# Staging tiles of two triangular inverses, the order of four tiles, and eighteen first convolution taps, in a one-core decoder layer

## The chip, the cores and the metric

The kernel runs on one core of a Trainium2 chip. The core has a matrix engine (TensorE, "PE" in the profile; its weight loads are shown apart as "PEld"), a vector engine (VectorE, "DVE"), an activation engine (ScalarE, "ACT"), GpSimd ("POOL") and SyncE ("SP"), which here issues the DMA transfers. Each engine runs its own instructions in the order in which the built program lists them, and waits on semaphores for the others. The metric is the time of one execution in microseconds; lower is better.

## The reference, cut to what matters

One decoder layer for a sequence of 1024 positions with 1024 channels. A combined projection of the modulated input feeds two mixers: a recurrent branch (convolution of width 4, RG-LRU, times a GeLU gate) and a Gated DeltaNet of 16 value heads on 8 key heads in chunks. Then follow merge gates, an output projection and a gated MLP. The parts that the change touches are these:

```python
def causal_dwconv(x, w):
    """Depthwise causal conv. x: (B, S, C), w: (K, C); y[t] = sum_k w[k] * x[t-K+1+k]."""
...
def chunk_gated_delta_rule(q, k, v, g, beta):
    ...
    kb = k * beta[..., None]
    A = jnp.where(strict, jnp.einsum('bhnid,bhnjd->bhnij', kb, k) * decay, 0.0)
    T = A + jnp.eye(c, dtype=F32)
    u = lax.linalg.triangular_solve(T, v * beta[..., None], left_side=True, lower=True)
    w = lax.linalg.triangular_solve(T, kb * jnp.exp(G)[..., None], left_side=True, lower=True)
...
def token_mixer(h, w_in, rg_conv_w, rg_conv_b, ...):
    proj = h @ w_in
    xr, gr, q, k, v, z, a_in, b_in, g_a, g_b = split_cols(proj, IN_SPLITS)
    xr = causal_dwconv(xr, rg_conv_w) + rg_conv_b
```

The triangular solves are done in the kernel by computing the inverses of unit triangular blocks of 64 x 64.

## The kernel before, in words

Every large product is made of matmuls of 128x512 outputs, three for each pair of tiles: each operand is split into a rounded part and a remainder, and lines 267, 268 and 269 multiply high by high, low by high and high by low. A weight tile is loaded by `load_w` (L254: a DMA into `wr`, a rounded copy `wh` on ACT, the remainder `wl` on DVE, both in the split helper, L200 and L201). One projection of a 128-channel tile takes 48 such matmuls, and its two halves go to two PSUM tiles of the tag `mm`, of which the first phase has four (L404). A PSUM tile is taken again only when its last reader is done.

The program has two phases up to the output projection. The first works through a list `ORDER` (L638 to L656): K is a key head, G a merge gate, Z an output gate of a value head, X a recurrent tile. It begins G K G K Z K G K, then Z K G K Z K G K, then X Z G X Z and so on, with the RG-LRU pieces (`lru`) between the X. The second phase (from L658) makes queries q and values v by the same projections and runs the chunks of the delta rule.

A key head (`key_head`, L490) projects, convolves with four taps on DVE (`conv`, L304: the first tap at L307, or at L309 where there is a bias, the others at L312), multiplies the tile with itself in 16 pieces on PE (L503, PSUM tag `pre`), scales the products on DVE (L509) and writes 64x64 blocks to DRAM (L518). An output gate (`z_steps`, L624) takes each half of a projection from PSUM through a tanh on ACT (L628, tile `th`) and a multiplication on DVE (L629, tile `z`), and stores it.

After every fourth key head `invert(b)` (L523) is emitted. It loads the blocks of eight heads as one tile `tri` (L527), 128 blocks of 64x64 with a block on each partition, and inverts them by 62 steps of two DVE instructions each (L531 into `tmp`, L533 back into `tri`). Then it clears the other triangle (L538, L540), stores the inverse (`inv_d`, L541), and also stores the transposed inverse: eight pieces `tmpT` of 64x512, copied alternately by ACT (L550) and DVE (L548), each followed by its DMA (L551).

What sets the order: a framework's scheduler decides the order of each engine's list when the program is built, from the program's order, priorities and the buffers. `invert` is emitted under `tc.high_priority(offset=-30000)` (L655), which lets its instructions be placed behind others. Each tile belongs to a tag with a fixed number of buffers, a ring, and a tile waits for the last use of the tile that had its buffer before. The rings that matter: `tri` and `tmp` of `tri_pool`, and the ring of half tiles (`half(...)`, 128x512, tag "hf") with four buffers in the first phase. From that ring come `sq`, `hi`, `lo` (the norm of a key, L337 and L345), `sg` (L560), `th` and `z` (L627). Large tiles (`g(...)`) come from a common area; when `tri_pool` is closed (L659) its place is free for the second phase, whose tiles `kT` (key heads loaded again) and `x` (inverses) are made in `beside_load` and `inverse_load`.

Of the kernel before, what the change touches and what calls it, by code (L numbers as in the profile page):

```python
# [9 lines left out]
F32 = mybir.dt.float32  # L10
F32R = mybir.dt.float32r
AF = mybir.ActivationFunctionType
# [4 lines left out]
P = 128  # L17
D = 1024
S = 1024
# [6 lines left out]
QKH = 8  # L26
VH = 16
CH = 128
NCH = S // CH
BK = 64  # L30
# [3 lines left out]
TJ = 8  # L34
# [56 lines left out]
def hybrid_layer_kernel(ctx: ExitStack, tc: tile.TileContext, xT, c, w_adaT, cols_in, rows_in,  # L91
                        w_in, w_ab, w_rg, w_pa, w_pb, w_out, w_gu, w_dn, out):
    nc = tc.nc
    V, A, G, T, DMA = nc.vector, nc.scalar, nc.gpsimd, nc.tensor, nc.sync
    uid = [0]

    def nm(s):
        uid[0] += 1
        return f"{s}_{uid[0]}"
# [12 lines left out]
    def g(shape=(P, S), dt=F32, name="g"):  # L112
        tag, bufs = cur["rings"].get(name, ("g", cur["g"]))
        t = cur["pool"].tile([P, S + 4], dt, tag=tag, bufs=bufs, name=nm(name))
        n = math.prod(shape[1:])
        t = t[0 : shape[0], 0:n]
        return t if len(shape) == 2 else t.rearrange("p (a b) -> p a b", a=shape[1])

    def half(name, dt=F32):
        return cur["pool"].tile([P, HALF], dt, tag="hf", bufs=cur["hf"], name=nm(name))  # L120
# [4 lines left out]
    def ct(shape, dt=F32, name="c"):  # L125
        return const.tile(list(shape), dt, name=nm(name))
# [3 lines left out]
    def col(name, i):  # L130
        o = COL[name] + i
        return cols[:, o : o + 1]
# [4 lines left out]
    tri_pool = tri_stack.enter_context(tc.tile_pool(name="tri_pool", bufs=1))  # L137
# [20 lines left out]
    def cst(v, name):  # L158
        t = ct([P, 1], name=name)
        G.memset(t, v)  # L160
        return t
# [3 lines left out]
    eps_rms = cst(4.0 * RMS_EPS, "eps_rms")  # L165
    eps_ln = cst(LN_EPS / (ALPHA * ALPHA), "eps_ln")
    floor = cst(SQRT_FLOOR, "floor")


    ada = ct([P, 48], name="ada")  # L170
# [128 lines left out]
    def conv_in():  # L299
        t = g((P, S + 4), name="cv")  # L300
        V.memset(t[:, 0:4], 0.0)
        return t

    def conv(t, taps, wcol, out_t, bias=None):  # L304
        o = 4 - (taps - 1)
        if bias is None:
            V.tensor_scalar(out=out_t, in0=t[:, o : o + S], scalar1=wcol(0), scalar2=None, op0=ALU.mult)  # L307
        else:
            V.tensor_scalar(out=out_t, in0=t[:, o : o + S], scalar1=wcol(0), scalar2=bias,  # L309
                            op0=ALU.mult, op1=ALU.add)  # L310
        for i in range(1, taps):
            V.scalar_tensor_tensor(out=out_t, in0=t[:, o + i : o + i + S], scalar=wcol(i), in1=out_t,  # L312
                                   op0=ALU.mult, op1=ALU.add)

    def silu2(x, th):

        A.activation(th, x, AF.Tanh, scale=0.5)
        V.scalar_tensor_tensor(out=x, in0=th, scalar=1.0, in1=x, op0=ALU.add, op1=ALU.mult)

    def qkv_tile(j):  # L320

        res = []
        for _ in qkv_steps(j, res):
            pass
        return res[0]

    def qkv_steps(j, res):
        cv = conv_in()
        yield from project_steps(
            w_in[T_Q + j], lambda ps, hf: A.activation(cv[:, 4 + hf * HALF : 4 + (hf + 1) * HALF], ps, AF.Copy))  # L330
        t = g(name="qkv")
        conv(cv, 4, lambda i: col("qkv_w", j * 4 + i), t)
        silu2(t, cv[:, 0:S])
        res.append(t)

# [44 lines left out]
    first_cv = {}  # L380
    with tc.tile_pool(name="ps_first", bufs=1, space=PSUM, reuse_waits="tile") as psf:
# [11 lines left out]
        for i in range(NFIRST):  # L393
            t = conv_in()
# [95 lines left out]
    def key_head(i):  # L490
        j = QKH + i
        if i in first_cv:
            t = g(name="k")
            conv(first_cv[i], 4, lambda q: col("qkv_w", j * 4 + q), t)
            silu2(t, first_cv[i][:, 0:S])
        else:
            t = qkv_tile(j)
        scale_by_norm(t, eps_l2, 1.0)
        DMA.dma_start(out=kT_d[i], in_=t)
        kk = [pre_ps() for _ in range(2)]  # L500
        for cc in range(NCH):
            s = t[:, cc * CH : (cc + 1) * CH]
            T.matmul(kk[cc // 4][:, (cc % 4) * CH : (cc % 4 + 1) * CH], s, s, start=True, stop=True)  # L503
        decs = [decay_rows(2 * i + hh) for hh in range(2)]
        ns = [d.rearrange("p (c i) -> p c i", c=NCH) for d in decs]
        for q in range(2):
            for hh in range(2):
                for cc in range(4 * q, 4 * q + 4):
                    V.scalar_tensor_tensor(  # L509
                        out=ns[hh][:, cc, :], in0=kk[q][:, (cc % 4) * CH : (cc % 4 + 1) * CH],  # L510
                        scalar=nbeta[:, cc, 2 * i + hh : 2 * i + hh + 1], in1=ns[hh][:, cc, :],
                        op0=ALU.mult, op1=ALU.mult)
        for hh in range(2):
            h = 2 * i + hh
            b, r = h // 8, h % 8
            n = ns[hh]
            for bl in range(2):
                DMA.dma_start(  # L518
                    out=blk_d[b][bl * BK + r * NCH : bl * BK + (r + 1) * NCH].rearrange("c j i -> j c i"),
                    in_=n[bl * BK : (bl + 1) * BK, :, bl * BK : (bl + 1) * BK])  # L520
            DMA.dma_start(out=off_d[h], in_=n[0:BK, :, BK : 2 * BK])

    def invert(b):  # L523

        flat_m = tri_pool.tile([P, BK * (BK + 1)], F32, tag="tri", name=nm("tri"))
        m = flat_m[:, 0 : BK * BK].rearrange("p (k i) -> p k i", k=BK)
        DMA.dma_start(out=m, in_=blk_d[b])  # L527
        for j in range(1, BK - 1):
            w = BK - 1 - j
            tmp = tri_pool.tile([P, 1024], F32, tag="tmp", name=nm("tmp"))[:, 0 : j * w].rearrange("p (k i) -> p k i", k=j)  # L530
            V.tensor_tensor(out=tmp, in0=m[:, 0:j, j : j + 1].to_broadcast([P, j, w]),  # L531
                            in1=m[:, j : j + 1, j + 1 :].to_broadcast([P, j, w]), op=ALU.mult)
            V.tensor_tensor(out=m[:, 0:j, j + 1 :], in0=m[:, 0:j, j + 1 :], in1=tmp, op=ALU.add)  # L533

        n = BK // 2
        while n:
            low = flat_m.rearrange("p (b x) -> p b x", x=2 * n * (BK + 1))[:, :, BK * n : 2 * BK * n]
            V.memset(low.rearrange("p b (r c) -> p b r c", c=BK)[:, :, :, 0:n], 0.0)  # L538
            n //= 2
        V.memset(flat_m[:, 0 : BK * BK : BK + 1], 1.0)  # L540
        DMA.dma_start(out=inv_d[b], in_=m)  # L541
        ts = tri_pool.tile([P, 1024], F32, tag="tmp", name=nm("tmpT"))[0:BK]
        for q in range(BK // TJ):
            o = q * TJ * BK % 1024
            t = ts[:, o : o + TJ * BK].rearrange("p (j k) -> p j k", j=TJ)
            src = m[0:BK, :, TJ * q : TJ * (q + 1)].rearrange("p k j -> p j k")
            if q % 2:
                V.tensor_copy(out=t, in_=src)  # L548
            else:
                A.activation(t, src, AF.Copy)  # L550
            DMA.dma_start(out=invT_d[b][:, TJ * q : TJ * (q + 1), :], in_=t)  # L551
# [18 lines left out]
    def xr_tile(t):  # L570
        cv = conv_in()
        project(w_in[T_XR + t], lambda ps, hf: A.activation(cv[:, 4 + hf * HALF : 4 + (hf + 1) * HALF], ps, AF.Copy))
        x = g(name="xr")
        conv(cv, 4, lambda i: col("rg_w", t * 4 + i), x, bias=col("rg_b", t))
        xr32[t] = x
        xrh[t], xrl[t] = split_hi_lo(x, "xr")

# [97 lines left out]
            T.matmul(psd[0:BK, cc * BK : (cc + 1) * BK], s[:, cc, :], x[BK:P, cc, BK : 2 * BK], start=True, stop=True)  # L675
        A.activation(x[0:BK, :, BK : 2 * BK], psd[0:BK, :].rearrange("p (c i) -> p c i", c=NCH), AF.Copy)

    def inverse_load(h):

        b, r = h // 8, h % 8  # L680
        x = g((P, NCH, CH), name="x")
        V.memset(x[BK:P, :, 0:BK], 0.0)
        parts = sm([BK, 2, HALF], tag="inv", bufs=2, name="inv")
        n_off, yT = (parts[:, q, :].rearrange("p (c i) -> p c i", c=NCH) for q in range(2))
        DMA.dma_start(out=n_off, in_=off_d[h])
        DMA.dma_start(out=yT, in_=invT_d[b][r * NCH : (r + 1) * NCH].rearrange("c j k -> j c k"))
        for bl in range(2):
            DMA.dma_start(out=x[bl * BK : (bl + 1) * BK, :, bl * BK : (bl + 1) * BK],
                          in_=inv_d[b][bl * BK + r * NCH : bl * BK + (r + 1) * NCH].rearrange("c j i -> j c i"))
        return x, n_off, yT  # L690
# [15 lines left out]
    def projections(i, st):  # L706

        yield from qkv_steps(i, st["q"])
        for h in (2 * i, 2 * i + 1):
            yield from qkv_steps(2 * QKH + h, st["v"])  # L710

    def beside_load(i, st):
        st["k"] = g(name="kT")
        DMA.dma_start(out=st["k"], in_=kT_d[i])
        st["inv"] = [inverse_load(h) for h in (2 * i, 2 * i + 1)]
        st["x"] = [v[0] for v in st["inv"]]

    def beside(i, st):

# [165 lines left out]
        yield from branch_b_steps()  # L885

    sts = [{"q": [], "v": []} for _ in range(QKH)]
    beside_load(0, sts[0])
    for _ in projections(0, sts[0]):
        pass  # L890
# [272 lines left out]
    for gi, fs in enumerate(groups):  # L1163
# [3 lines left out]
        for hf in range(NHALF) if ends else (0,):  # L1167
# [9 lines left out]
            if hf == 0:  # L1177
                steps(ln, 99)
                if gi == len(groups) - 1:
                    ln, _ = down_and_norm(fs, acts, (0, 0, HALF))  # L1180
# [85 lines left out]
```

## Time and profile before

| | us |
|---|---|
| three runs, median (lowest to highest) | 2544.42 (2543.34 to 2545.72) |
| the profiled execution, its own time | 2544.34 |
| its span, first to last instruction | 2542.6 |
| PE busy in the span | 2391.7 (94%) |
| DVE busy | 1637.3 (64%) |
| ACT busy | 1108.0 (44%) |
| inverse 0, first L531 to last L533 | 201.3 to 451.5 |
| inverse 1, first L531 to last L533 | 479.9 to 711.4 |

The profile's page gives each engine's busy time and share of the span; a table in 40 slices of 63.6 us; the chain of work that ended last; and groups of instructions by line. A group's row reads: line, engine, operation, output tile <- input tiles, shape, count, then busy us and mean ns of one, then the idle time of that engine just before them, and what ended it. A row of the timeline reads: start, length, engine, line, operation, names, count, and in brackets the idle time before it and who released it. Rows of the windows give the busy time of each engine in a stretch, with the count of its instructions, and then the granted clock of TensorE as a share of full speed.

### The profile page before, as it was taken

The page shows a single profiled execution, that of the slowest core. Times are in us where ns is not written, and L with a number is a line of the kernel's source. Part 1 is how long each engine was busy: PE and PEld are TensorE (multiplying, and loading weights), DVE is VectorE, ACT ScalarE, POOL GpSimd, SP SyncE. Part 2 cuts the span into 40 slices and gives each one's busy share as a digit, 9 for nine tenths or more (in the row PEclk, how much of TensorE's full clock was granted, in tenths as well). Part 3 has the DMA queues.
Part 4 walks back from the last instruction along what each step waited for, and adds up shares of the span by engine and source line. Part 5 has one row for each costly group of instructions (what it writes and reads, how often), then busy time and mean ns, then how long its engine had stood idle before and what let it go on. Part 6 is the DMA issues. An engine that isn't in the chain of part 4 may idle for free.

```text
span 2542.6 us, 30275 instructions
## 1 busy us (share of the span) xinstructions
PE 2391.7 (94%) x11591; PEld 1972.7 (78%) x11591; DVE 1637.3 (64%) x2624; ACT 1108.0 (44%) x1554; POOL 165.1 (6%) x135
## 2 busy tenths in 40 slices
PE   6989999999858999999998989999999999999997
PEld 4877887788647887778877778878788888888877
DVE  6778999799955667766666346655674234335565
ACT  5556445534634555665555322224543122113354
POOL 3000000000000001000010000004000000000304
PEclk9999999999979999999999999999999999999998
DMA  7356422522261233232334368562232111123233
GB/s 271 120 145 191 120 88 82 178 77 94 75 166 55 83 96 107 81 99 85 94 129 158 103 209 291 187 216 91 83 100 75 51 50 49 51 75 97 94 124 108
DMA packets 163233, 295.47 MB, mean 116 GB/s; under 512 B 63760, under 2 KB 74384, under 8 KB 162576
## 3 DMA queue, kind: packets, MB, share of 16 engines
q1 hardware_dynamic: 163088, 293.54, 36.6%
q8 instruction: 91, 1.49, 0.2%
q14 instruction: 54, 0.44, 0.1%
HBM read 233.65 MB, written 55.64 MB: 114 GB/s over the span
## 4 chain that ended last, share of the span: by engine, by line
PE 73%; DVE 8%; ACT 7%; DMA 3%; issue 3%; SPq 1%; POOL 0%; ACTq 0%; DVEq 0%; POOLq 0%
PE mm L267 22%; PE mm L268 22%; PE mm L269 22%; DMA wada<-in_w_adaT 1%; DVE wl L201 1%; ACT wh L200 1%; PE pv L790 1%; PE pso L811 1%; DMA xraw<-xr 1%; ACT L353 1%; PE pd L799 1%; PE pso L812 1%; ACT L354 1%; PE pre L675 1%; PE pre L669 1%
## 5 line engine op out<-in xcount | busy, mean ns | idle before, releaser
L267 PE MATMUL mm<-h,wh 128*128 128x512 f32 x1424 | 581.7, 409 | 41.9 <-ACT cv L330 32.2
L267 PE MATMUL mm<-hi,wh 128*128 128x512 f32 (+1 forms) x1536 | 586.4, 384 | 15.3 <-ACT hi L200 11.1
L268 PE MATMUL mm<-lo,wh 128*128 128x512 f32 (+1 forms) x1536 | 586.7, 383 | 0.0
L269 PE MATMUL mm<-hi,wl 128*128 128x512 f32 (+1 forms) x1536 | 583.1, 383 | 3.4 <-DVE wl L201 3.4
L269 PE MATMUL mm<-h,wl 128*128 128x512 f32 x1424 | 559.9, 395 | 3.3 <-DVE wl L201 3.3
L268 PE MATMUL mm<-h,wh 128*128 128x512 f32 x1424 | 561.1, 394 | 0.1
L200 ACT ACTIVATE wh<-wr 128x1024 fp32r<-128x1024 f32 (+3 forms) x251 | 254.2, 1014 | 635.7 <-PE mm L268 588.4
L201 DVE TENSOR_TENSOR wl<-wr,wh 128x1024 fp32r<-128x1024 f32 (+3 forms) x251 | 297.4, 1185 | 165.0 <-ACT wh L200 162.0
L267 PEld LDWEIGHTS mm<-hi,wh 128*128 128x128 f32 x1536 | 290.8, 189 | 75.8 <-ACT hi L200 13.6
L267 PEld LDWEIGHTS mm<-h,wh 128*128 128x128 f32 x1424 | 271.9, 191 | 95.3 <-ACT cv L330 32.8
L269 PEld LDWEIGHTS mm<-hi,wl 128*128 128x128 f32 x1536 | 290.7, 189 | 60.7 <-DVE wl L201 5.2
L268 PEld LDWEIGHTS mm<-lo,wh 128*128 128x128 f32 x1536 | 290.9, 189 | 57.3 <-DVE lo L201 1.7
L269 PEld LDWEIGHTS mm<-h,wl 128*128 128x128 f32 x1424 | 270.4, 190 | 64.1 <-DVE wl L201 5.2
L268 PEld LDWEIGHTS mm<-h,wh 128*128 128x128 f32 x1424 | 271.7, 191 | 50.3 <-DVE h L201 0.6
L1129 DVE SCALAR_TENSOR_TENSOR y<-mm,mods,y 128x512 f32<-128x512 f32 (+1 forms) x56 | 37.7, 674 | 153.7 <-PE mm L269 153.7
L760 POOL TENSOR_TENSOR kg<-kT,eg 128x256 f32<-128x256 f32 x49 | 50.1, 1023 | 1300.5 <-ACT eg L758 1249.1
L312 DVE SCALAR_TENSOR_TENSOR qkv<-cv,cols,qkv 128x1024 f32<-128x1024 f32 x87 | 114.2, 1313 | 0.7
L531 DVE TENSOR_TENSOR tmp<-tri 128x62 f32<-128x62 f32 (+30 forms) x124 | 106.3, 857 | 5.2 <-DMA tri<-blk_d 3.7
L533 DVE TENSOR_TENSOR tri<-tri,tmp 128x62 f32<-128x62 f32 (+30 forms) x124 | 106.2, 856 | 1.9
L355 DVE TENSOR_TENSOR qkv<-qkv,rs 128x1024 f32<-128x1024 f32 x29 | 35.6, 1226 | 55.9 <-ACT rs L354 55.9
L201 DVE TENSOR_TENSOR lo<-sq,hi 128x512 fp32r<-128x512 f32 x64 | 43.9, 686 | 40.9 <-PE pre L350 20.8
L1105 DVE SCALAR_TENSOR_TENSOR gate<-cv,cols,gate 128x512 f32<-128x512 f32 x88 | 67.2, 763 | 2.7
(272 smaller groups left out, 2895.9 us busy)
## 6 DMA issues: line engine op xcount, KB each, us to landing
wr<-in_w_in SPq DMA_DIRECT2D x81, 512.0 KB, 3.7
wr<-in_w_gu SPq DMA_DIRECT2D x74, 512.0 KB, 3.6
wada<-in_w_adaT SPq DMA_DIRECT2D x64, 256.0 KB, 5.5
wr<-in_w_dn SPq DMA_DIRECT2D x22, 512.0 KB, 3.5
wada<-in_w_adaT SPq DMA_DIRECT2D x16, 512.0 KB, 5.9
decay<-row_d SPq DMA_DIRECT2D x16, 512.0 KB, 6.0
z_d<-z SPq DMA_DIRECT2D x32, 256.0 KB, 2.8
gb<-row_d SPq DMA_DIRECT2D x64, 128.0 KB, 3.5
```

Source lines behind the costliest of these rows:

```text
L200: A.activation(hi, src, AF.Copy)
L201: V.tensor_tensor(out=lo, in0=src, in1=hi, op=ALU.subtract)
L267: T.matmul(ps, w[0][:, kk, :], xh, start=first, stop=False)
L268: T.matmul(ps, w[0][:, kk, :], xl, start=False, stop=False)
L269: T.matmul(ps, w[1][:, kk, :], xh, start=False, stop=last)
L312: V.scalar_tensor_tensor(out=out_t, in0=t[:, o + i : o + i + S], scalar=wcol(i), in1=out_t, op0=ALU.mult, op1=ALU.add)
L355: V.tensor_tensor(out=t, in0=t, in1=rs, op=ALU.mult)
L531: V.tensor_tensor(out=tmp, in0=m[:, 0:j, j : j + 1].to_broadcast([P, j, w]), in1=m[:, j : j + 1, j + 1 :].to_broadcast([P, j, w]), op=ALU. ...
L533: V.tensor_tensor(out=m[:, 0:j, j + 1 :], in0=m[:, 0:j, j + 1 :], in1=tmp, op=ALU.add)
L760: (G if i else V).tensor_tensor(out=kg, in0=two(st["k"][:, s]), in1=eg, op=ALU.mult)
L1105: V.scalar_tensor_tensor(out=t, in0=cv[:, 2 + i : 2 + i + HALF], scalar=col("ffn_w", 3 * f + i), in1=t, op0=ALU.mult, op1=ALU.add)
L1129: evac = V.scalar_tensor_tensor(out=ys[d][hf][:, t], in0=ps, scalar=mods[:, 24 + d : 25 + d], in1=ys[d][hf][:, t], op0=ALU.mult, op1=ALU.a ...
```

## The change

It has three parts.

1. The eight pieces `tmpT` of a transposed inverse, which were two halves of one 128x1024 tile of the tag `tmp` of `tri_pool`, are now eight tiles `half("tmpT")`, from the ring of four half tiles that the first phase also uses for `sq`, `hi`, `lo`, `sg`, `th` and `z`.
2. The tiles `kT` and `x` of the first two key heads are allocated at the start of the second phase, key by key, ahead of all its other tiles; `inverse_load` is given its `x` tile.
3. The first tap of the convolution of the eight keys and ten recurrent tiles, 18 instructions of 128x1024, goes to ACT as an activation with the tap as its scale and the bias (or a constant tile `zero`) as its bias. The queries and values keep theirs on DVE.

```diff
+    zero = cst(0.0, "zero")
...
-    def conv(t, taps, wcol, out_t, bias=None):
+    def conv(t, taps, wcol, out_t, bias=None, on_act=False):
         o = 4 - (taps - 1)
-        if bias is None:
+        if on_act:
+            A.activation(out_t, t[:, o : o + S], AF.Identity, scale=wcol(0), bias=zero if bias is None else bias)
+        elif bias is None:
             V.tensor_scalar(out=out_t, in0=t[:, o : o + S], scalar1=wcol(0), scalar2=None, op0=ALU.mult)
...
-        conv(cv, 4, lambda i: col("qkv_w", j * 4 + i), t)
+        conv(cv, 4, lambda i: col("qkv_w", j * 4 + i), t, on_act=j >= QKH and j < 2 * QKH)
...
-            conv(first_cv[i], 4, lambda q: col("qkv_w", j * 4 + q), t)
+            conv(first_cv[i], 4, lambda q: col("qkv_w", j * 4 + q), t, on_act=True)
...
-        ts = tri_pool.tile([P, 1024], F32, tag="tmp", name=nm("tmpT"))[0:BK]
         for q in range(BK // TJ):
-            o = q * TJ * BK % 1024
-            t = ts[:, o : o + TJ * BK].rearrange("p (j k) -> p j k", j=TJ)
+            t = half("tmpT")[0:BK, 0 : TJ * BK].rearrange("p (j k) -> p j k", j=TJ)
             src = m[0:BK, :, TJ * q : TJ * (q + 1)].rearrange("p k j -> p j k")
...
-        conv(cv, 4, lambda i: col("rg_w", t * 4 + i), x, bias=col("rg_b", t))
+        conv(cv, 4, lambda i: col("rg_w", t * 4 + i), x, bias=col("rg_b", t), on_act=True)
...
-    def inverse_load(h):
+    def inverse_load(h, x):
         b, r = h // 8, h % 8
-        x = g((P, NCH, CH), name="x")
...
+    def beside_tiles(st):
+        if "x" not in st:
+            st["k"] = g(name="kT")
+            st["x"] = [g((P, NCH, CH), name="x") for _ in range(2)]
+
     def beside_load(i, st):
-        st["k"] = g(name="kT")
+        beside_tiles(st)
         DMA.dma_start(out=st["k"], in_=kT_d[i])
-        st["inv"] = [inverse_load(h) for h in (2 * i, 2 * i + 1)]
-        st["x"] = [v[0] for v in st["inv"]]
+        st["inv"] = [inverse_load(2 * i + hh, st["x"][hh]) for hh in range(2)]
...
     sts = [{"q": [], "v": []} for _ in range(QKH)]
+    for st in sts[0:2]:
+        beside_tiles(st)
     beside_load(0, sts[0])
```

The change moves instructions that no line of the diff names. Three places matter. In the rows below a name's number tells one tile from another, and the changed kernel's line numbers are 3 higher than before's around `invert` (L531 is L534, L533 is L536, L548 is L549, L550 is L551, L503 is L506, L628 is L629, L629 is L630).

**DVE, inverse 0.** Before, the steps of the inversion stand among the other work of the first phase. `qkv_1864` is a key's tile, `decay` the decay rows of the next key, `wl` a weight's remainder:

```order
L531 TENSOR_TENSOR tmp_1319<-tri_1317 128x62
L538 MEMSET tri_1317 128x32x32
...
L540 MEMSET tri_1317 128x64
L485 TENSOR_SCALAR decay_1698<-decay_1698,gcum_587 128x128 x8
L485 TENSOR_SCALAR decay_1709<-decay_1709,gcum_587 128x128 x8
L312 SCALAR_TENSOR_TENSOR qkv_1864<-cv_1804,cols_63,qkv_1864 128x1024
L533 TENSOR_TENSOR tri_1317<-tri_1317,tmp_1319 128x62
L201 TENSOR_TENSOR wl_2164<-wr_2162,wh_2163 128x1024
L509 SCALAR_TENSOR_TENSOR decay_1698<-pre_1688,nbeta_585,decay_1698 128x128 x4
```

In the changed kernel nothing stands between them, from the first L534, right behind the last scaling of key 3 (L512), through all 124 to the last copy of the transposed inverse; only then follows the output gate of the first Z of the second group (`z_1570`), and inverse 1 has the same form:

```order
L512 SCALAR_TENSOR_TENSOR decay_1286<-pre_1266,nbeta_587,decay_1286 128x128 x4
L534 TENSOR_TENSOR tmp_1321<-tri_1319 128x62
...
L534 TENSOR_TENSOR tmp_1504<-tri_1319 128x62
L536 TENSOR_TENSOR tri_1319<-tri_1319,tmp_1504 128x62
L549 COPY tmpT_1536<-tri_1319 64x512
L630 SCALAR_TENSOR_TENSOR z_1570<-th_1571,mm_1545 128x512
L630 SCALAR_TENSOR_TENSOR z_1600<-th_1601,mm_1575 128x512
L202 TENSOR_TENSOR lo_1676<-sq_1673,hi_1675 128x512
```

What moved: the DVE instructions of the two inversions, 124 steps, seven memsets and four copies each, came together into two uninterrupted runs, ahead of the output gates `z_1570` and, behind inverse 1, `z` of the next Z.

**PE, behind key 3's products (L503, then L506).** Before, the projection of key 5 (`mm_1812`) has begun ahead of them and goes on behind them:

```order
L268 MATMUL mm_1812<-h_142,wh_1807 128x512
L269 MATMUL mm_1812<-h_141,wl_1808 128x512
L503 MATMUL pre_1263<-qkv_1231 128x128 x4
L503 MATMUL pre_1264<-qkv_1231 128x128 x4
L267 MATMUL mm_1812<-h_164,wh_1807 128x512
L268 MATMUL mm_1812<-h_165,wh_1807 128x512
```

In the changed kernel the projection of key 5 (`mm_1821`) begins behind them:

```order
L270 MATMUL mm_1785<-h_262,wl_1753 128x512
L506 MATMUL pre_1265<-qkv_1233 128x128 x4
L506 MATMUL pre_1266<-qkv_1233 128x128 x4
L268 MATMUL mm_1821<-h_120,wh_1816 128x512
L269 MATMUL mm_1821<-h_121,wh_1816 128x512
L270 MATMUL mm_1821<-h_120,wl_1817 128x512
```

The tile `mm_1821` has the PSUM buffer of `mm_1545`, which is read by `th_1571` and `z_1570`: the first matmul of key 5 waits for `z_1570`. Behind key 7's products it is the same with the last three matmuls of a merge gate between: the first projection of X waits for the `z` behind inverse 1.

**ACT, at the end of the first phase.** `cv_5356` and, in the changed kernel, `cv_5375` take query 0's projection from PSUM. Before, the four ACT copies of inverse 1 stand ahead of it:

```order
L616 ACTIVATE e_5318<-e_5318,floor_99 128x1024
L200 ACTIVATE wh_5493<-wr_5492 128x1024
L550 ACTIVATE tmpT_2566<-tri_2370 64x512 x4
L330 ACTIVATE cv_5356<-mm_5364 128x512
L330 ACTIVATE cv_5356<-mm_5390 128x512
```

In the changed kernel they are long past (they stand together, ahead of the `th` of the output gate, at each inverse):

```order
L617 ACTIVATE e_5334<-e_5334,floor_99 128x1024
L201 ACTIVATE wh_5512<-wr_5511 128x1024
L333 ACTIVATE cv_5375<-mm_5383 128x512
L333 ACTIVATE cv_5375<-mm_5409 128x512
L320 ACT_TABLE_LOAD
```

From query 0's projection on, the lists of the engines are practically the same in both kernels.

## The prediction

> **What bounds the kernel now.** I read the page's busy times first, then a table of windows by stage, then the waits of PE, and last the timelines around the two inversions.
>
> ```profile
> span 2542.6 us, 30275 instructions
> PE 2391.7 (94%) x11591; PEld 1972.7 (78%) x11591; DVE 1637.3 (64%) x2624; ACT 1108.0 (44%) x1554; POOL 165.1 (6%) x135
> ```
>
> PE is busy for 94% of the span. What a change can win is PE's idle time, 151 us in all, and what it can lose is any new stop of PE. The windows show where the idle time lies (the last two numbers are DMA's share and GB/s, and the one before them is TensorE's granted clock):
>
> ```profile
> core 0: us, PE busy (x) PEld busy (x) DVE busy (x) ACT busy (x) POOL busy (x), PEclk, DMA share, GB/s
> 178.00:287.00 109.00, 105.24 (x495) 87.15 (x494) 96.69 (x220) 63.11 (x79) 0.00 (x0) 0.98 0.58 169
> 287.00:695.00 408.00, 396.54 (x1713) 323.19 (x1711) 375.86 (x417) 200.60 (x232) 0.00 (x0) 0.99 0.32 99
> 695.00:735.00 40.00, 7.82 (x22) 6.07 (x22) 24.05 (x37) 9.66 (x10) 0.00 (x0) 0.57 0.54 153
> 735.00:1430.00 695.00, 650.30 (x3854) 544.20 (x3853) 443.03 (x784) 390.82 (x649) 50.15 (x49) 0.99 0.33 100
> 325.00:390.00 65.00, 65.00 (x288) 53.61 (x287) 63.39 (x61) 33.32 (x40) 0.00 (x0) 1.00 0.24 76
> ```
>
> From 178 to 695 us, the stretch in which both inversions are computed, PE is idle for only 3.8 + 11.5 = 15.2 us, though DVE is 89% and 92% busy. The inversions are woven into DVE's free time and PE hardly notices them. The last row gives the price of one matmul at full clock with no idle time: 65 / 288 = 0.226 us. Between 695 and 735 us PE does almost nothing. The waits and the timeline name that hole:
>
> ```profile
> PE mm L267 <- ACT cv L330: 32.2, 1, 32.2
> 694.75 0.39 PE L269 MATMUL mm<-h,wl 128*128 128x512 f32 x1
> 711.44 1.07 ACT L550 ACTIVATE tmpT<-tri 64x512 f32<-64x512 f32 x1 [12.08 <-DVE tri L533]
> 725.73 1.06 ACT L550 ACTIVATE tmpT<-tri 64x512 f32<-64x512 f32 x1 [2.35 <-DMA invT_d<-tmpT]
> 726.70 1.05 ACT L330 ACTIVATE cv<-mm 128x512 f32<-128x512 f32 x2
> 727.32 0.80 PE L267 MATMUL mm<-h,wh 128*128 128x512 f32 x1 [32.18 <-ACT cv L330]
> 727.92 0.63 PE L268 MATMUL mm<-h,wh 128*128 128x512 f32 x1
> 733.46 0.40 PE L269 MATMUL mm<-h,wl 128*128 128x512 f32 x1
> ```
>
> Query 0's products are done at 695, but the ACT copy that frees their PSUM tile stands in ACT's list behind four copies `tmpT`. These wait for the last step of inverse 1 (711), and then, one after the other, for the DMA that frees the half they write. PE stands for 32.2 us, and after that it is slow: from 727.32 to 733.46 the matmuls start 0.427 us apart instead of 0.226, 14.4 in 6.1 us, a loss of about 3 us.
>
> **The change part by part.** *The tiles kT and x first.* In the built program they lie where they lay before, all places being moved by the 32 bytes of the new constant. So nothing waits for anything else than before, and I cost it at 0; what covers it is that the second phase's lists are the same from query 0 on.
>
> *The first taps on ACT.*
>
> ```profile
> L307 DVE TENSOR_SCALAR qkv<-cv,cols 128x1024 f32<-128x1024 f32 x29 | 21.7, 748 | 5.7 <-ACT cv L330 5.7
> L309 DVE TENSOR_SCALAR xr<-cv,cols 128x1024 f32<-128x1024 f32 x10 | 8.1, 808 | 0.8 <-ACT cv L572 0.8
> L238 ACT ACTIVATE xk<-xk,adab,mods 128x1024 f32<-128x1024 f32 x8 | 9.9, 1240 | 20.2 <-DVE adab L179 20.2
> L200 ACT ACTIVATE h<-xk 128x1024 fp32r<-128x1024 f32 x8 | 8.5, 1059 | 0.3
> ```
>
> DVE loses 8 x 0.75 + 10 x 0.81 = 14.1 us. ACT gains 18 instructions of a kind not in the trace in this place. The nearest row with a scale and a bias read from tiles, L238, gives 1.24 us and a plain one 1.06, so 19 to 22 us; I take 22. ACT is about half busy from 178 to 695, so this is hidden, and if that cover were gone it would be 22 us.
>
> *The transposed inverse in half tiles* decides. The eight `tmpT` now share four buffers with `th` and `z`, and the order of the instructions answers this: each inversion stands on DVE as one run, the output gate's `z` stands right behind it, and the first matmul after key 3's (key 7's) products needs the PSUM tile that this `z` reads. So PE stops from the end of those products until the whole inversion is done. The length of an inversion that nothing interrupts follows from these rows:
>
> ```profile
> L531 DVE TENSOR_TENSOR tmp<-tri 128x62 f32<-128x62 f32 (+30 forms) x124 | 106.3, 857 | 5.2 <-DMA tri<-blk_d 3.7
> L533 DVE TENSOR_TENSOR tri<-tri,tmp 128x62 f32<-128x62 f32 (+30 forms) x124 | 106.2, 856 | 1.9
> L538 DVE MEMSET tri<- 128x1024 f32 (+5 forms) x12 | 3.9, 338 | 0.4 <-issue 0.3
> L548 DVE COPY tmpT<-tri 64x512 f32<-64x512 f32 x8 | 4.8, 602 | 15.8 <-DMA invT_d<-tmpT 15.6
> L629 DVE SCALAR_TENSOR_TENSOR z<-th,mm 128x512 f32<-128x512 f32 x32 | 21.8, 683 | 6.0 <-ACT th L628 3.8 <-PE pre L351 2.0
> 707.02 0.52 DVE L533 TENSOR_TENSOR tri<-tri,tmp 128x342 f32<-128x342 f32 x1
> 707.57 0.46 DVE L531 TENSOR_TENSOR tmp<-tri 128x290 f32<-128x290 f32 x1
> 708.07 0.46 DVE L533 TENSOR_TENSOR tri<-tri,tmp 128x290 f32<-128x290 f32 x1
> ```
>
> The groups hold both inversions, so one has (106.3 + 106.2) / 2 = 106.3 us of steps, 1.9 of memsets and 2.4 of copies. Where the steps already follow each other, at 707, some 0.035 us lie between one's end and the next one's start; 124 of these are 4.3 us. With the `z` behind, 0.7, the run takes 115.6 us. Its start follows from what key 3 does today:
>
> ```profile
> 178.54 1.95 PE L503 MATMUL pre<-qkv 128*128 128x128 f32 x16
> 183.53 2.15 DVE L509 SCALAR_TENSOR_TENSOR decay<-pre,nbeta,decay 128x128 f32<-128x128 f32 x8
> 190.10 0.33 SPq L527 DMA_DIRECT2D tri<-blk_d  x1
> tri<-blk_d SPq DMA_DIRECT2D x2, 2048.0 KB, 9.0
> blk_d<-decay SPq DMA_DIRECT2D x32, 128.0 KB, 2.7
> 284.51 1.95 PE L503 MATMUL pre<-qkv 128*128 128x128 f32 x16
> ```
>
> From the start of the products to the issue of the load of `tri` it is 190.10 - 178.54 = 11.6 us, and to its landing 9.0 more, 20.6 in all. The products take 1.9 of it. So PE stops for 20.6 - 1.9 + 115.6 = 134.3 us, from about 179 to 313 us (six matmuls of key 5, 1.4 us, now stand behind the stop and not ahead of it; this moves the stop and costs nothing). The second stop is of the same length, less three matmuls between (0.7), and plus about 1.3 us because one weight load now stands on SP's queue among key 7's block transfers: 134.9. Between them lies the work that took 284.5 - 180.5 = 104 us, so that the second stop runs from about 415 to 550 us. Queued behind the gate's `th` on ACT and `z` on DVE are the norms of the next key, and these find PE waiting with them; nothing else on PE could go ahead. Both ends: if L509 and the DMAs go faster on idle engines, 5 us less for each stop (the load's landing at 9.0 us with other loads beside it against 2.7 for a small one); if the tmpT copies inside the run wait for the DMA of a half, as their 15.6 us of idle time above allow, up to 8 us more for each.
>
> *Cold restarts.* Two new long stops end in the half-rate stretch that the row at 727.32 shows: +2 x 3.0 = 6.0 us. The page "TensorE: Matmul & The Clock Gate" of the Trainium skill says in Part 1, on the clock gate, that the array runs at half clock after an idle window of about 3.4 us and at full clock again after about as long a time busy. By that figure a restart would cost 1.7 us and the sum would be 1.3 lower, for two new ones less the one that goes; the 6.1 us at half rate that this trace shows are longer, and the sum goes by the trace.
>
> *The boundary.* ACT's four copies no longer stand ahead of query 0's evacuation. The 32.2 us and their cold restart, 3.0, go; what is late next is the last RG-LRU piece's chain on ACT, which stands there in either order, and I leave 3 us for it: -32. Ends: -35 if nothing is late, and 0 if another late tile holds the same place.
>
> *DVE relieved.* These are PE's waits from 178 to 695 us:
>
> ```profile
> PE mm L267 <- ACT wh L200: 4.6, 2, 3.5
> PE mm L269 <- DVE wl L201: 3.3, 2, 2.2
> PE pre L603 <- DVE xs L588: 2.6, 1, 2.6
> PE pre L350 <- ACT hi L200: 2.6, 2, 1.3
> ```
>
> Outside the two stops DVE has neither the inversions nor the taps, and weights and norms are split sooner. Of the 15.2 us of idle PE time between 178 and 695, with about 2 us of half clock behind them, I take 12 as gone (0 to 17).
>
> The sum against the profiled execution: 2544.3 + 134.3 + 134.9 + 6.0 - 32 - 12 = 2775.5. That execution is within 0.1 us of the median of the three runs, 2544.42, so **2775 us** it is, 9% slower.
>
> **The rivals.** *Only the good part comes: faster.* Should PE have enough products in its list that need no `z`, and run them beside the inversion, what is left is the boundary: 2544.3 - 35 = 2509 us. For it speaks the profile of before, in which inversions run for 250 us without any stop of PE. Against it speaks the order of the changed kernel: `z` behind the last copy, and PE's next matmul behind `z`. It decides if PE's wait behind key 3's products is under about 16 us per inversion. 3%.
>
> *Only one inversion stops PE.* Then one stop, its restart and half of the relief count: 2544.3 + 134.3 + 3.0 - 32 - 6 = 2644 us. For it speaks that behind key 7 the X tiles need no `z`; against it, that they need its PSUM tile. 5%.
>
> *The gains do not come.* The hole at the boundary is filled by another wait and PE's small idles stay, as the trace shows some of them (2.6 us for the RG-LRU's input) to come from chains and not from a full DVE: 2544.3 + 269.2 + 6.0 = 2820 us. Against it: the ACT row at 711.44 names the inversion alone as releaser, and it will be done 160 us earlier. 8%.
>
> *The change doesn't do what it says.* The reordering of the tiles moves none of them; this is already in the sum as 0.
>
> **How the numbers follow.** 84% for two full stops with the boundary's gain in whole or part, 8% for no gains, 5% for one stop, 3% for none. The main case's own ends: -10 and +16 for the stops, -3 and up to 32 at the boundary, -5 and +12 for the relief. These are not all late together, so the range is 2745 to 2812 us. A measurement of this kernel can tell about 0.2%, 5 us, from no change. Faster holds 3%, no change 1%, slower 96%.
>
> **What would show it.** In the profile of the changed kernel: two waits of PE for `z` of about 134 us, the first from about 179 us on; DVE rows of L534 and L536 back to back for some 110 us in each, and nothing else of DVE between them; half clock for some 6 us behind each stop; no wait of over 10 us for `cv` at the end of the first phase; a second part, from query 0's values on, as long as before (1815 us from 727.3 to the end). It is wrong if the first stop is shorter than 100 us, if PE runs matmuls while the steps run, or if the hole of 32 us remains.

## The result, and the profile after

The changed kernel takes 2760.73 us (median of 4 runs, 2759.47 to 2762.47), against 2543.88 us for the kernel before (4 runs, three of them those of the table above). The ratio is 1.085, with a 95% interval of 1.0836 to 1.0863: it is slower by 217 us. The forecast was 2775 us, with a range of 2745 to 2812.

The page's first lines of the changed kernel, and the engines' rows of its table in 40 slices (each digit a slice's busy share, or for PEclk the granted clock, in tenths):

```profile
span 2758.9 us, 30259 instructions
PE 2384.8 (86%) x11591; PEld 1969.4 (71%) x11591; DVE 1644.6 (60%) x2606; ACT 1130.3 (41%) x1573; POOL 164.8 (6%) x136
PE   6940580199999889999999899999999999999997
DVE  6769678745544656667666543666667424425465
PEclk9975795599999999999999999999999999999998
```

PE has as many instructions as before and is even busy for 7 us less (2384.8 against 2391.7), because fewer of them ran at half clock (of the matmuls with 512 columns 119 took 0.55 us or more, against 144 before). The span has grown around them. Two holes of PE, around the fourth slice and at the seventh and eighth, stand where DVE is busy. The list of PE's waits puts both down to one cause, and the timeline shows them (the brackets give the idle time and its releaser):

```profile
PE mm L268 <- DVE z L630: 265.4, 3, 132.5
PE mm L268 <- ACT gate L607: 5.3, 1, 5.3
```

```profile
169.38 2.05 PE L506 MATMUL pre<-qkv 128*128 128x128 f32 x16
303.93 0.80 PE L268 MATMUL mm<-h,wh 128*128 128x512 f32 x1 [132.50 <-DVE z L630]
404.39 1.95 PE L506 MATMUL pre<-qkv 128*128 128x128 f32 x16
539.43 0.80 PE L268 MATMUL mm<-h,wh 128*128 128x512 f32 x1 [132.40 <-DVE z L630]
930.92 0.80 PE L268 MATMUL mm<-h,wh 128*128 128x512 f32 x1 [5.35 <-ACT gate L607]
945.83 0.50 PE L268 MATMUL mm<-h,wh 128*128 128x512 f32 x1 [1.41 <-ACT cv L333]
```

Inside the first hole DVE does one thing, the inversion with its memsets and copies. Its timeline at the beginning and at the end of the run:

```profile
188.85 0.22 DVE L534 TENSOR_TENSOR tmp<-tri 128x62 f32<-128x62 f32 x1 [12.92 <-DMA tri<-blk_d]
...
302.10 0.26 DVE L534 TENSOR_TENSOR tmp<-tri 128x62 f32<-128x62 f32 x1
302.40 0.27 DVE L536 TENSOR_TENSOR tri<-tri,tmp 128x62 f32<-128x62 f32 x1
302.70 0.58 DVE L549 COPY tmpT<-tri 64x512 f32<-64x512 f32 x1
303.21 1.46 DVE L630 SCALAR_TENSOR_TENSOR z<-th,mm 128x512 f32<-128x512 f32 x2
```

From the first step at 188.85 to PE's restart at 303.93 it is 115.1 us, and from 424.36, where the second inversion starts, to 539.43 again 115.1. The windows between these marks show the rest:

```profile
core 0: us, PE busy (x) PEld busy (x) DVE busy (x) ACT busy (x) POOL busy (x), PEclk, DMA share, GB/s
172.00:304.00 132.00, 0.07 (x1) 0.07 (x1) 114.67 (x153) 5.41 (x6) 0.00 (x0) 0.51 0.12 35
304.00:407.00 103.00, 100.74 (x464) 83.31 (x464) 65.78 (x158) 64.02 (x78) 0.00 (x0) 0.98 0.51 160
407.00:540.00 133.00, 0.60 (x2) 0.50 (x2) 116.01 (x153) 6.30 (x7) 0.00 (x0) 0.51 0.12 35
550.00:910.00 360.00, 359.12 (x1579) 296.06 (x1578) 173.87 (x164) 181.38 (x209) 0.00 (x0) 1.00 0.29 86
946.00:2759.00 1813.00, 1737.55 (x8738) 1441.52 (x8738) 1020.48 (x1683) 735.80 (x1112) 144.60 (x115) 0.98 0.35 110
```

From 550 to 910 us PE is idle for 0.9 us, where before, woven together with the inversions, it was idle for 11.5 us of 408 (the wait of 5.35 us for `gate` at 930.92 lies behind that window). Cut at places that both kernels have, the 216.3 us between the two spans lie here:

| stretch | before, us | after, us | difference |
|---|---|---|---|
| start to key 3's products | 178.5 | 169.4 | -9.2 |
| to PE's next product | 1.7 | 134.6 | +132.9 |
| to key 7's products | 104.3 | 100.5 | -3.8 |
| to query 0's first product | 397.9 | 526.5 | +128.6 |
| to value 0's first product | 44.9 | 14.9 | -30.0 |
| to the end | 1815.3 | 1813.1 | -2.2 |

### The profile page after: what moved, and what is told of

It reads as the page before. It is cut to its first block, busy times and chain, and to the rows that moved or that the text cites. A ratio compares the mean times of both kernels' runs of the same rounds, so it can differ in the third digit from the quotient of the medians.

```text
span 2758.9 us, 30259 instructions
## 1 busy us (share of the span) xinstructions
PE 2384.8 (86%) x11591; PEld 1969.4 (71%) x11591; DVE 1644.6 (60%) x2606; ACT 1130.3 (41%) x1573; POOL 164.8 (6%) x136
## 4 chain that ended last, share of the span: by engine, by line
PE 65%; ACT 6%; DVE 5%; DMA 2%; issue 2%; SPq 0%; POOL 0%; DVEq 0%; ACTq 0%; POOLq 0%
PE mm L268 19%; PE mm L269 19%; PE mm L270 19%; DMA wada<-in_w_adaT 1%; DVE wl L202 1%; PE pv L794 1%; ACT wh L201 1%; PE pso L815 1%; PE pso L816 1%; PE pd L803 1%; ACT L356 1%; PE pre L676 1%; PE pre L670 1%; ACT L357 1%; ACT rs L356 1%
## 5 line engine op out<-in xcount | busy, mean ns | idle before, releaser
L534 DVE TENSOR_TENSOR tmp<-tri 128x62 f32<-128x62 f32 (+30 forms) x124 | 106.6, 859 | 29.6 <-DMA tri<-blk_d 25.5
L536 DVE TENSOR_TENSOR tri<-tri,tmp 128x62 f32<-128x62 f32 (+30 forms) x124 | 106.3, 857 | 4.0
L551 ACT ACTIVATE tmpT<-tri 64x512 f32<-64x512 f32 x8 | 8.7, 1082 | 241.3 <-DVE tri L536 241.3
```

## The experiments

The theory to be tested is that of the prediction: the transposed pieces share a ring with tiles of the running work, and through it the whole inversion comes to stand ahead of PE's next projection. Its rivals are these: the relief of DVE by the taps lets the steps run together; the ring is only too short; the stop is set by copies and DMAs. All times are medians, and ratios are to the kernel before on the same chip. Waits are given as the total, how often, and the longest, in us.

**The ring alone.** The kernel before with only this:

```diff
-        ts = tri_pool.tile([P, 1024], F32, tag="tmp", name=nm("tmpT"))[0:BK]
...
-            t = ts[:, o : o + TJ * BK].rearrange("p (j k) -> p j k", j=TJ)
+            t = half("tmpT")[0:BK, 0 : TJ * BK].rearrange("p (j k) -> p j k", j=TJ)
```

> The kernel before with the transposed inverse's eight pieces taken from the ring of half tiles, and nothing else of the change. Theory (the shared ring alone makes each inversion one run that PE waits for): two waits of PE for z of about 132 us each, no hole of 32 us at the end of the first phase; without the taps' relief 5 to 15 us above the changed kernel, so 2765 to 2776 us. Rival (the taps' relief of DVE lets the steps run together, the ring is harmless): inversions woven in as before, 2505 to 2545 us.

2768.01 us (4 runs; ratio 1.088, 1.0864 to 1.0897). PE's waits in it:

```profile
PE mm L267 <- DVE z L627: 264.7, 2, 132.4
PE mm L267 <- ACT gate L604: 3.6, 1, 3.6
```

The two stops are there without any tap moved. The rival that the taps do it falls. Key 3's products start at 177.66 us here and at 169.38 in the full change, so most of the 7 to 9 us by which the full change is faster come from the taps, before the first stop.

**The taps and the tiles without the ring.** The changed kernel with the inverse's pieces as before:

```diff
+        ts = tri_pool.tile([P, 1024], F32, tag="tmp", name=nm("tmpT"))[0:BK]
...
-            t = half("tmpT")[0:BK, 0 : TJ * BK].rearrange("p (j k) -> p j k", j=TJ)
+            o = q * TJ * BK % 1024
+            t = ts[:, o : o + TJ * BK].rearrange("p (j k) -> p j k", j=TJ)
```

> The changed kernel with the transposed inverse's pieces again as two halves of a tile of tag tmp: the first taps on ACT and the order of the tiles remain. Theory (the stops come from the shared ring, the relief of DVE from the taps): no wait of over 10 us for z; the first part up to key 3's products 5 to 9 us shorter as in the changed kernel; inverse 1 ends some 14 us earlier, so that the hole at the end of the first phase is about 18 us and not 32; 2518 to 2534 us. Rival (the taps bring nothing because DVE was hidden): 2540 to 2548 us.

2514.21 us (4 runs; ratio 0.9892, 0.9872 to 0.9912), 28 us faster than before and 4 us below the range that was expected. PE's waits up to 1000 us hold none for `z` of that size, and the hole at the end of the first phase is the longer of these two waits:

```profile
PE mm L268 <- ACT cv L333: 14.2, 2, 14.1
```

The last step of inverse 1, which ended at 711.4 us, now ends at 684.5; that is 27 us, though only 14.1 us of DVE work were taken away. 7.9 of the 27 lie already before key 3's products (170.66 against 178.54). From these products to the end of the last step DVE is busy for 465.4 us and not 488.0; 10.4 of these 22.6 us are taps, and most of the rest is work of the last recurrent piece that now stands behind the last step. The hole of 32.2 us became 14.1, and its end, value 0's first product, came from 727.32 to 700.47 us.

**The tiles alone.** The kernel before with `kT` and `x` allocated first:

```diff
+    for st in sts[0:2]:
+        beside_tiles(st)
     beside_load(0, sts[0])
```

> The kernel before with the tiles kT and x of two key heads allocated first in the second phase, and nothing else but the constant tile. Theory (no tile moves, every engine's list is the same as before): no difference, within 0.2% of before, 2539 to 2549 us. Rival (other places or waits): more than 5 us either way.

2544.93 us (10 runs; ratio 1.0005, 0.9996 to 1.0015): no difference that can be measured. The tiles move nothing here, so the 28 us above are put down to the taps.

**A longer ring.** The changed kernel with six half tiles:

```diff
-    first = phase("first", 17, 4)
+    first = phase("first", 17, 6)
```

> The changed kernel with six buffers and not four in the first phase's ring of half tiles. Theory (it is enough that tiles of the running work follow low-priority tiles in one ring): the runs stay whole, both waits of about 132 us stay, 2750 to 2768 us. Rival (the ring is only too short for eight pieces): the waits go or are cut by half, under 2650 us.

2766.54 us (2 runs; ratio 1.0873, 1.0851 to 1.0895). PE waits for `z` twice, 128.6 and 132.5 us:

```profile
PE mm L268 <- DVE z L630: 261.1, 2, 132.5
```

Two more buffers do not help. Six are still fewer than the eight pieces, so it is not shown what a shared ring of eight or more would do; that no such length is needed is shown by the ring of two below.

**Half of the inversion.** The changed kernel without steps 32 to 62 of each inversion, so that its inverses are unfinished:

```diff
-        for j in range(1, BK - 1):
+        for j in range(1, BK // 2):
```

> The changed kernel with only steps 1 to 31 of the 62 of each inversion; steps 32 to 62, which have as many elements, are left out, and the transposed copies of the second half of the columns come right behind. Theory (PE's stop is the inversion's length on DVE): each stop is shorter by half of 106.6 + 106.3 us over two inversions and 62 gaps of 0.035, that is 53.2 + 2.2 = 55.4 us, less some us for copies that wait for a half's DMA; so 2 x 55.4 = 111 less, 2650 to 2660 us. Rival (the stop is set by the copies, their DMAs or the load of tri): under 30 us less, 2730 to 2761 us.

2663.95 us (2 runs), 97 us less than the changed kernel and 4 to 14 above the expected values. The stops:

```profile
256.36 0.79 PE L268 MATMUL mm<-h,wh 128*128 128x512 f32 x1 [83.80 <-DVE z L630]
443.25 0.80 PE L268 MATMUL mm<-h,wh 128*128 128x512 f32 x1 [84.19 <-DVE z L630]
...
249.16 0.59 DVE L549 COPY tmpT<-tri 64x512 f32<-64x512 f32 x1 [0.55 <-DMA invT_d<-tmpT]
255.61 0.69 DVE L630 SCALAR_TENSOR_TENSOR z<-th,mm 128x512 f32<-128x512 f32 x1 [5.86 <-ACT th L629]
...
254.98 0.60 ACT L629 ACTIVATE th<-mm 128x512 f32<-128x512 f32 x1 [4.88 <-DMA invT_d<-tmpT]
```

Each stop is 48.5 us shorter; 55.4 were taken out. So most of the stop is the inversion's own length on DVE, and not the copies, their DMAs or the load of `tri`. The missing 7 come from the shared ring as well: four copies now fall together at the end, `th` waits for the DMA that frees one of the four half tiles (4.88 us), and `z` waits for `th` (5.86 us). In the full inversion the two `th` run at 296.3 and 298.7. The second waits 1.84 us for such a DMA, but both are done before the last step begins at 302.1, and only the steps count.

**A ring of their own.** The changed kernel with the pieces in two half tiles that nothing else uses:

```diff
-            t = half("tmpT")[0:BK, 0 : TJ * BK].rearrange("p (j k) -> p j k", j=TJ)
+            t = tri_pool.tile([P, HALF], F32, tag="tT", bufs=2, name=nm("tmpT"))[0:BK, 0 : TJ * BK].rearrange("p (j k) -> p j k", j=TJ)
```

> The changed kernel with the eight pieces in a ring of their own, two buffers of 128x512. Theory (sharing with th and z does the harm, the early copies are good): steps woven in as before, no wait of over 10 us for z, and the copies spread over the inversion, so that the hole of 32 us at the end of the first phase shrinks to under 8 us; with the taps' relief 2497 to 2518 us. Rival (pieces that wait for two buffers' DMAs hold up DVE and ACT in the middle of the running work): 2530 us or more.

2507.85 us (4 runs; ratio 0.987, 0.9854 to 0.9887). One tag differs from the changed kernel, and the time is 253 us lower: the stops are gone, the steps are woven in, and the copies stand between them and not at the end. But the hole is still 11.1 us, and not under 8 as was expected. PE's wait and the timeline on ACT:

```profile
PE mm L268 <- ACT cv L333: 11.1, 1, 11.1
680.40 1.15 ACT L617 ACTIVATE e<-e,floor 128x1024 f32<-128x1024 f32 x1 [3.17 <-DVE e L615]
681.45 1.04 ACT L201 ACTIVATE wh<-wr 128x1024 fp32r<-128x1024 f32 x1
689.46 1.09 ACT L333 ACTIVATE cv<-mm 128x512 f32<-128x512 f32 x2 [6.96 <-DMA rec_d<-gr]
```

The inversion is done at 669 here, and still the evacuation of query 0 waits, for the store of the last recurrent piece's `gr`: the second phase's `cv` lies where first-phase tiles were.

**The own ring without taps.** The same edit on the kernel before.

> The kernel before with the eight pieces in a ring of their own, two buffers of 128x512, and neither taps nor tiles. Theory: the steps of inverse 1 still end late (711 us before), but the last copies no longer wait for each other's DMAs and ACT's stand ahead of query 0's evacuation no more; the hole goes from 32 us to under 12, 2518 to 2534 us; the taps are worth the difference from the kernel with both, 5 to 20 us. Rival (the hole comes from the inversion's end and not from the copies): 2540 us or more.

2534.0 us (12 runs; ratio 0.9969, 0.9958 to 0.9979), 8 us faster than before. The hole is 13.6 us, more than the 12 expected, and again ends on the store of `gr`; the inversion's last step is at 708.6:

```profile
PE mm L267 <- ACT cv L330: 15.0, 2, 13.6
709.80 1.08 ACT L330 ACTIVATE cv<-mm 128x512 f32<-128x512 f32 x2 [7.52 <-DMA rec_d<-gr]
```

With taps and tiles the own ring is 26 us faster, more than the 5 to 20 expected. But not all of this is the taps' direct work: up to value 0's first product it is 20.3 us (710.45 against 690.11). Some 7 us lie in the second product behind it, whose 48 matmuls take 18.1 us here and 10.9 there, because PE waits for a query's norm (2.8 us) and for a `cv` (1.4 us) and runs at half clock behind them. None of the 18 taps is there, and why the order differs stays open.

**And `cv` in the triangles' place.** The own ring with taps, and the first two `cv` of the second phase allocated ahead of `kT` and `x`:

```diff
     def qkv_steps(j, res):
-        cv = conv_in()
+        cv = ahead.pop(0) if ahead else conv_in()
...
+    ahead += [conv_in(), conv_in()]
     for st in sts[0:2]:
         beside_tiles(st)
```

> The kernel with the taps on ACT and a ring of their own for the transposed pieces, and besides it the first two convolution inputs cv of the second phase allocated ahead of kT and x, so that they lie in the triangles' place and not where the last recurrent piece's gr and its neighbours were. Theory (what is left of the hole is query 0's evacuation waiting for the store of the last gr): PE's wait of 11.1 us for cv shrinks to under 5, since the triangle is free by about 677 us and ACT by 682.5; 6 to 10 us less than the 2507.9 of the own ring, 2497 to 2503 us. Rival (ACT's chain of the last recurrent piece holds the evacuation anyway, or kT and x now come late): 2505 us or more.

2501.47 us (5 runs; ratio 0.9835, 0.9821 to 0.9848). The same place on ACT, and what PE waits:

```profile
681.50 1.04 ACT L201 ACTIVATE wh<-wr 128x1024 fp32r<-128x1024 f32 x1
682.45 1.06 ACT L335 ACTIVATE cv<-mm 128x512 f32<-128x512 f32 x2
...
683.08 0.79 PE L268 MATMUL mm<-h,wh 128*128 128x512 f32 x1 [4.02 <-ACT cv L335]
```

The evacuation no longer waits for the store, and PE's wait goes from 11.1 to 4.0 us. This is the fastest kernel of the study, 1.65% faster than the one before: all three ideas of the change, the early copies, the taps and the tiles allocated first, are in it, with another ring and another tile put first.

## Why the prediction was right

*The stops.* Forecast 134.3 and 134.9 us, measured 132.5 and 132.4. The run of the inversion was worked out as 115.6 us from the groups and the gap between steps, and measured 115.1. The lead was 1.1 us shorter than the rows of before gave: the load of `tri` was issued 11.1 us after the products' start, not 11.6, and the first step began 8.4 us after that issue, not 9.0. The copies inside the run cost no waiting, one of the two ends that were kept; `th` had its half tile in time. Behind key 7 `tri` was issued 11.7 us after the products' start, so the weight load on SP's queue cost 0.6 us and not 1.3. That the two inversions would stop PE was read from the order of the built program; that the shared ring makes this order is shown by the two runs with the ring alone and with an own ring.

*Cold restarts.* Forecast 3.0 us each, measured 1.9. The matmuls of the changed kernel's two restarts:

```profile
303.93 0.80 PE L268 MATMUL mm<-h,wh 128*128 128x512 f32 x1 [132.50 <-DVE z L630]
307.51 0.53 PE L270 MATMUL mm<-h,wl 128*128 128x512 f32 x1
307.88 0.40 PE L268 MATMUL mm<-h,wh 128*128 128x512 f32 x1
...
543.01 0.54 PE L270 MATMUL mm<-h,wl 128*128 128x512 f32 x1
543.38 0.39 PE L268 MATMUL mm<-h,wh 128*128 128x512 f32 x1
```

Nine starts in 3.95 us, at full rate 2.03, so 1.9 lost, both times. The 6.1 us of the kernel before was one sample, and I took it for the size of all. The rule of the Trainium skill that I set aside (page "TensorE: Matmul & The Clock Gate", Part 1: about 3.4 us at half clock, in a window that does not start with the kernel) was nearer to these two restarts than that row. With the ring alone two stops of the same length ended in 5.25 and 4.84 us at half rate, so 3.95 is no fixed size either.

*The boundary.* Forecast -32: the wait of 32.2 us and its restart of 3.0 gone, and 3 us left for what is next late. Measured are -30.0 between query 0's and value 0's first products, and the restart of 3.0, which lay behind value 0's first product, is gone too: -33.0. But the last recurrent piece's chain, named as next late, is late just ahead of this stretch: PE waits 5.35 us for `gate`, where before it was 0.65. With these 4.7 us the boundary brought -28.3.

*DVE relieved.* Here is the term that was off in size. From 178 to 695 us I counted 12 us. Measured there, with the second stop, the restarts (1.9 each) and six matmuls that moved in (1.4) taken out of the table's third and fourth stretch, it is about 12.8. That this is so near is partly luck: the 4.7 us of the longer wait for `gate` lie in it, and without them it is 17.5, at the upper end of the 0 to 17. And the stretch ahead of it was left at nothing, and it won 9.2 us, of which 1.4 are the six matmuls that moved out. The waits of PE up to 178 us were there to be read in the kernel before:

```profile
PE pre L351 <- DVE lo L201: 3.8, 1, 3.8
PE pre L350 <- ACT hi L200: 3.4, 1, 3.4
```

Both are in a key's norm, behind DVE's taps of the first keys, and neither is in the changed kernel or in the one with the taps but without the ring: 7.2 us. The term was worked out from the windows in which the inversions lie, and the taps of keys 0 to 3 lie before them.

*The sum.* 231.2 forecast, 216.3 measured between the spans. The difference of 14.9 is 7.8 for the first stretch, 4.3 for the stops, 2.2 for the restarts, 1.0 at the boundary (-33.0) and 0.8 for the relief (12.8), less 0.8 by which the rest behind value 0's first product is longer, and less 0.4 for the end of key 3's products, which no longer overlaps the next matmul.

*The rivals.* Both stops came, so neither "only the good part" nor "one inversion" did. The first of these, 2509 us, is what the own ring gave (2507.85), but that is a coincidence: there the hole shrank by 21 us and not by all of 32, and the relief of DVE, which that sum leaves out, gave the rest. That the reordered tiles move nothing was right, and measured.

## What to carry to other kernels

Work that a scheduler is to weave in behind other work should not share a ring of buffers with that work. Here one tag was worth 253 us: with a shared ring the whole inversion stood ahead of the tiles of the running work that follow it in the ring. How the scheduler comes to this order was not looked into. Before a buffer is saved that way, the order of the built program tells it, on the engine that runs the low-priority work and on the one that waits.

The share of an engine's busy time says little about what a relief of it is worth. DVE was busy 64% of the span, and 14.1 us less of it gave 28 us: about 18 in the one hole of PE that a chain of DVE's work had ended (32.2 us became 14.1), and 7.9 in waits ahead of it. Count from the first instruction that is moved, not from where the trouble is seen.

## What the runs showed of the hardware that was not expected

TensorE's half-rate stretch is not of one length after an idle time: 6.1 us after 32.2 us of idle (before), 3.95 us after 132.5 and after 132.4 us, and 4.86 after 5.35 us (changed); with the ring alone it was 5.25 and 4.84 us after 132.4 and 132.3 us. The length of the idle time does not set it. In the records of the granted clock of both kernels each stretch at full or half clock lasts a multiple of 3.41 us (133.12 us twice in the changed kernel, that is 39 times), but for the one that the end of the run cuts off: the lengths fit a clock that changes only on such a grid, on which the stops' ends fall at different places.

One price was left open between 1.06 and 1.24 us and is now measured. The first tap as an activation with scale and bias read from tiles took what the nearest row gave, 1241 to 1252 ns in the mean of its three groups, against 1240; the largest group:

```profile
L308 ACT ACTIVATE xr<-cv,cols 128x1024 f32<-128x1024 f32 x10 | 12.4, 1244 | 0.3
```

The steps of the inversion ran no faster on a DVE with nothing else to do and with little DMA about (a share of 0.12 in both stops): 859 and 857 ns in the mean, against 857 and 856 woven in.
